# A routed expert layer in which the expert that ranks last by load has no slots of its own

## The chip, the cores and the metric

The kernel runs on one core of one Trainium2 chip. The metric is device microseconds (us) for one execution of the whole program. All times below come from three timed runs of the kernel before and from one profiled execution of it.

## The reference, cut to what matters

The program computes two transformer-like blocks on 256 tokens of width 1024. The change concerns the end of the first block, a layer of 32 experts of which each token uses four:

```python
N_EXPERTS, TOP_K, D_EXPERT = 32, 4, 1024
logits = xt @ w_router + b_router              # 256 tokens x 32 experts
top_logits, top_idx = lax.top_k(logits, TOP_K)
top_w = softmax(top_logits)
# for every expert e, on the tokens that chose it:
gate, up = split(xb @ w_gu[e] + b_gu[e], 2)    # 1024 x 2048 weights, 8 MB
act = (min(gate, 7) * sigmoid(1.702 * gate)) * (clip(up, -7, 7) + 1)
y_e = act @ w_dn[e] + b_dn[e]                  # 1024 x 1024 weights, 4 MB
# y[token] = sum over its four experts of top_w * y_e
```

How many of the 1024 (token, expert) pairs fall to an expert is known only when the router has run. The inputs are drawn from a fixed seed. After the experts come a layer norm and the second block (a pooling layer, a gated delta-rule layer, two wide multilayer perceptrons).

## The kernel before, in words

The program is a long straight line of instructions with one small loop in it. Its stages are: the token mixer of the first block, the router, the experts, and the second block.

**Ranks.** `route` (L680) counts the tokens of each expert and ranks the experts by that count (`rank`, L715). Expert 0 is always given rank 0, so that its weights can be loaded before the router has run. The row `eid` (L721) holds the expert of each rank; the load queue on SP reads one entry of it for each expert (L1080) and fetches that expert's weights by that number. So the order of the work is fixed when the program is built, in terms of ranks, and only the addresses are found at run time.

**Slots.** Each rank has a fixed number of token slots, `cap` (L966): 64 for rank 0, 128 for rank 1, 96 for ranks 2 to 4, 64 for ranks 5 to 14 and 32 for ranks 15 to 31. The text calls an expert by its rank and its slots. An expert with more tokens than slots leaves the rest to a general loop (`For_i`, L1122), which does one pass of 128 slots for each leftover piece, one piece after the other. How many passes there are (`n_over`, L768) and for which experts is found by `leftovers` (L747): `tier` compares the rank with each bound, `base` is the number of slots of the rank, and `f` says whether the count is above it.

**Order.** `_phase_b` (L955) spreads the four kinds of rank evenly over the sequence (`want`, L968) and packs neighbours into units of at most 128 slots (L972). A unit's tokens are gathered together: 32 matmuls with one-hot matrices (L800, L801) make the columns of all its experts. In the sequence below a bar ends a unit:

```
0 | 15 5 16 | 17 6 18 | 1 | 7 19 20 | 8 21 | 2 22 | 9 23 | 10 24 25 | 3 | 11 26 27 | 12 28 | 13 29 | 4 30 | 14 31
```

**One step of the sequence** (loop at L1070) puts on TensorE: the gate and up projection of this expert (`ex_gu`, L844, eight loads of 1 MB each), between its loads the scatter of the expert two steps back (L945) and the activation of the last one (transposes, L864 and L868); then the down projection of the last expert (`ex_down`, L920, four loads of 1 MB), and, when this expert is the first of its unit, the gather for the next unit between these loads.

**Matmul shapes.** An expert with 32 slots uses 32 of the array's 128 columns, so four matmuls run side by side; with 64 slots two run side by side. A 96-slot expert does its gate and up projection as three 32-slot pieces and its down projection one matmul at a time. A 128-slot expert does everything one matmul at a time.

**Loads.** All expert weights go through the one queue on SP into a ring of seven 1 MB buffers (`wpools`, L960). A load is issued when the matmuls of the load seven places earlier are done. Every expert has twelve loads, whatever its slots.

After the last step come the rest of its work, the general loop, and the second block.

Of the kernel before, what the change touches and what calls it, by code (L numbers as in the profile page):

```python
# [9 lines left out]
F32 = mybir.dt.float32  # L10
# [4 lines left out]
OP = mybir.AluOpType  # L15
AX = mybir.AxisListType
# [5 lines left out]
TT = 2  # L22
OFF = -1500
N_TOP, N_BIG = 2, 5
NL = 8
FB = 1
FE = 18
# [8 lines left out]
NO = 3  # L36
N_MID = 10
# [16 lines left out]
class K:  # L54
# [625 lines left out]
    def route(self, pb, p1, first):  # L680

        nc, sm = self.nc, self.sm
        E = N = 32
        wr, br, iota1, pcol = self.rt
        lg, W, M = self.lg, self.W, self.M
        iotaE = self.iotaE
        self.show("lg", lg)
        self.show("Wt", W)

        for tt in range(TT):  # L690
            pp = self.bank([128, N])
            if tt:
                nc.tensor.matmul(pp, self.ones, M[:, 0], start=True, stop=False)
            nc.tensor.matmul(pp, self.upper, M[:, tt], start=tt == 0, stop=True)
            nc.vector.scalar_tensor_tensor(p1[:, tt], pp, 1.0, M[:, tt], op0=OP.add, op1=OP.mult)

        pc = self.bank([N, E + 32])
        for tt in range(TT):
            nc.tensor.matmul(pc[:, :E], self.ones[:, :N], M[:, tt, :E], start=tt == 0, stop=tt == 1)
        for tt in range(TT):  # L700
            nc.tensor.matmul(pc[:, E:], M[:, tt], self.ones[:, :32], start=tt == 0, stop=tt == 1)
        next(first)
        key = self.t(pb, [N, E], F32, "key")
        nc.vector.scalar_tensor_tensor(key, pc[:, :E], 32.0, iotaE[:N, :E], op0=OP.mult, op1=OP.subtract)

        nc.vector.memset(key[:, 0:1], 1e6)
        cc = self.t(pb, [N, 1], F32, "cc")
        nc.vector.tensor_copy(cc, pc[:, E:E + 1])
        kc = self.t(pb, [N, 1], F32, "kc")
        nc.vector.scalar_tensor_tensor(kc, cc, 32.0, pcol, op0=OP.mult, op1=OP.subtract)  # L710
        nc.vector.memset(kc[0:1], 1e6)
        gt = self.t(pb, [N, E], F32, "gt")
        rank = self.t(pb, [N, 1], F32, "rank")
        nc.vector.tensor_scalar(gt, key, kc, None, op0=OP.is_gt)
        nc.vector.tensor_reduce(rank, gt, axis=AX.X, op=OP.add)  # L715
        PP = self.t(pb, [N, 2, E], F32, "PP")
        nc.vector.tensor_scalar(PP[:, 0], iotaE[:N, :E], rank, None, op0=OP.is_equal)
        pe = self.bank([1, E])
        nc.tensor.matmul(pe, pcol, PP[:, 0], start=True, stop=True)
        eid = self.t(pb, [1, 2, E], I32, "eid")  # L720
        nc.vector.tensor_copy(eid[:, 0], pe)  # L721
        fin(first)
        pT = self.t(pb, [N, 2, T], F32, "pTr")
        tab = self.t(pb, [128, 4, TT, E], F32, "tab")

        def permute(z, pos, less=None):

            pr = self.bank([128, 2, TT, E])
            for tt in range(TT):
                for q in range(2):  # L730
                    x = pT[:, 1] if q else pos
                    nc.tensor.matmul(pr[:, q, tt], x[:, tt * 128:tt * 128 + 128], PP[:, z], start=True,
                                     stop=q > 0 or less is None)
                    if q == 0 and less is not None:
                        nc.tensor.matmul(pr[:, q, tt], less[0], less[1], start=False, stop=True)
            nc.vector.tensor_copy(tab[:, 2 * z:2 * z + 2], pr)

        def by_rank():

            ptp = self.bank([N, 2, T])  # L740
            for tt in range(TT):
                nc.tensor.transpose(ptp[:, 0, tt * 128:tt * 128 + 128], p1[:, tt], self.ident)
                nc.tensor.transpose(ptp[:, 1, tt * 128:tt * 128 + 128], W[:, tt], self.ident)
            nc.vector.tensor_copy(pT, ptp)
            permute(0, pT[:, 0])

        def leftovers():  # L747

            tier = self.t(pb, [N, 4], F32, "tier")
            for q, n in enumerate((N_TOP, N_BIG, N_BIG + N_MID, 1)):  # L750
                nc.vector.tensor_scalar(tier[:, q:q + 1], rank, float(n), None, op0=OP.is_lt)
            base = self.t(pb, [N, 1], F32, "base")
            nc.vector.tensor_reduce(base, tier[:, 0:3], axis=AX.X, op=OP.add)
            nc.vector.scalar_tensor_tensor(base, tier[:, 3:4], -2.0, base, op0=OP.mult, op1=OP.add)
            nc.vector.tensor_scalar(base, base, 32.0, 32.0, op0=OP.mult, op1=OP.add)
            f = self.t(pb, [N, 2], F32, "f2")
            nc.vector.tensor_tensor(f[:, 0:1], cc, base, op=OP.is_gt)
            nc.vector.scalar_tensor_tensor(f[:, 1:2], cc, -128.0, base, op0=OP.add, op1=OP.is_gt)
            yield
            pn = self.bank([N, 4])  # L760
            nc.tensor.matmul(pn[:, 0:2], self.upper[:N, :N], f, start=True, stop=True)
            nc.tensor.matmul(pn[:, 2:4], self.ones[:N, :N], f, start=True, stop=True)

            b = self.t(pb, [N, 4], F32, "ib")
            nc.vector.tensor_copy(b, pn)
            nc.vector.tensor_tensor(b[:, 1:2], b[:, 1:2], b[:, 2:3], op=OP.add)
            self.n_over = self.t(pb, [1, 1], I32, "nover")
            nc.vector.tensor_tensor(self.n_over, b[0:1, 2:3], b[0:1, 3:4], op=OP.add)  # L768
            nc.vector.scalar_tensor_tensor(b[:, 0:2], b[:, 0:2], 1.0, f, op0=OP.add, op1=OP.mult)
            P2 = self.t(pb, [N, E], F32, "P2")  # L770
            nc.vector.tensor_scalar(P2, iota1[:N, :E], b[:, 1:2], None, op0=OP.is_equal)
            nc.vector.scalar_tensor_tensor(PP[:, 1], iota1[:N, :E], b[:, 0:1], P2, op0=OP.is_equal, op1=OP.add)
            pos = self.s4([N, T])
            nc.vector.tensor_scalar(pos, pT[:, 0], base, None, op0=OP.subtract)
            less = self.s4([N, 128])
            nc.vector.memset(less, -128.0)
            yield
            pe = self.bank([1, E])
            nc.tensor.matmul(pe, pcol, PP[:, 1], start=True, stop=True)
            nc.vector.tensor_copy(eid[:, 1], pe)  # L780
            permute(1, pos, (less, P2))
            yield
        return pT, PP, eid, tab, by_rank, leftovers
# [171 lines left out]
    def _phase_b(self, st, keep):  # L955
        nc, tc, i = self.nc, self.tc, self.i
        E = 32
        pb = self.pb = st.enter_context(tc.tile_pool(name="pb", bufs=1))
# [5 lines left out]

        order = []
        size = lambda r: 64 if r == 0 else 128 if r < N_TOP else 96 if r < N_BIG else 64 if r < N_BIG + N_MID else 32  # L966
        tiers = [range(0, 1), range(1, N_BIG), range(N_BIG, N_BIG + N_MID), range(N_BIG + N_MID, E)]
        want = [(WA + WB * (j + 0.5) / len(rs)) if n == 1 else (j + 0.5) / len(rs) for n, rs in enumerate(tiers)  # L968
                for j in range(len(rs))]
        flat = [(r, size(r)) for rs in tiers for r in rs]  # L970
        order = [flat[j] for j in sorted(range(E), key=lambda j: (flat[j][0] > 0, want[j]))]
        units, cur = [order[:1]], []  # L972
        for r, cap in order[1:]:
            if sum(c for _, c in cur) + cap > XC:
# [77 lines left out]
        def start():  # L1052

            for tt in range(TT):
                for h in range(2):
                    po = self.bank([128, 512])
                    nc.tensor.matmul(po, pT[:E, 1, tt * 128:tt * 128 + 128], bdn[:, h * 512:h * 512 + 512],
                                     start=True, stop=True)
                    s5 = slice(h * 512, h * 512 + 512)
                    nc.vector.tensor_tensor(po, po, self.g2[:, s5], op=OP.mult)  # L1060
                    nc.vector.scalar_tensor_tensor(ytok[:, tt, s5], ytok[:, tt, s5], ALPHA1, po, op0=OP.mult, op1=OP.add)
                yield

        def others():
            yield from leftovers()
            self.gdn_consts()
            yield
        pend, prev, old, left, pre = [start()] + [iter(())] * NO + [others()], None, None, E, self.pre_c(keep)
        late = []
        for u in range(len(units)):  # L1070
            items = nxt
            for n, (r, cap, xe, off, ow) in enumerate(items):
# [4 lines left out]
                if r:  # L1077

                    with tc.issue_after(self.mid):
                        e = nc.sync.value_load(eid[0:1, 0, r:r + 1], min_val=0, max_val=E - 1)  # L1080
                x = {"n": E - 1 - left}
                fills = []
                if prev:
                    fills = [self.ex_act(prev[0], prev[2], prev[4])]
# [25 lines left out]
                old, prev = prev, (x, e, cap, ow, bcol[:, :, r])  # L1110
        if old:
            fin(self.ex_scatter(old[0], old[2], old[3]))
        x, e, cap, ow, bg = prev
# [788 lines left out]
```

## Time and profile before

| what | value |
|---|---|
| three timed runs, median (lowest to highest) | 2034.7 us (2030.83 to 2046.16) |
| the profiled execution, its own time | 2035.08 us |
| its span from first to last instruction | 2032.3 us |
| busy share of the span: TensorE, VectorE, ScalarE, GpSimd | 91%, 48%, 32%, 1% |
| bytes read from HBM | 575.53 MB |
| mean granted TensorE clock | 0.945 |

The profiled execution lies 2.8 us above its span and 0.4 us above the median. Times inside the program are given from the start of the span. A matmul in float32 shows as two records in the trace, so 8 records of L844 are the four matmuls of one 1 MB load of a 32-, 64- or 128-slot expert, and 24 those of a 96-slot expert. [...]

### The profile page before, as it was taken

The numbers are of one execution on the slowest core, as the hardware profiler recorded it, in microseconds if no ns is written. First come the engines' busy times: TensorE is split into PE (matmuls) and PEld (weight loads), VectorE is DVE, ScalarE is ACT, GpSimd is POOL, SyncE is SP. The second block draws the span as 40 slices with busy tenths as digits, with TensorE's granted clock in tenths as the row PEclk, the third lists the DMA queues.
The fourth block names the chain that finished last, engine by engine and source line by source line (L and its number), as shares of the span: only waits on it lengthen the run. The fifth ranks groups of instructions, "written<-read, shape, count | busy, mean of one in ns | idle before, by whom it ended". The sixth has DMA issues, their size and how long they took to land. (4 is left out here: it accounts for less than half of the span.)

```text
span 2032.3 us, 28434 instructions
## 1 busy us (share of the span) xinstructions
PE 1841.4 (91%) x10991; PEld 1149.6 (57%) x10991; DVE 976.5 (48%) x2179; ACT 647.3 (32%) x1188; POOL 25.0 (1%) x53
## 2 busy tenths in 40 slices
PE   5999989988997899869988898799998899999998
PEld 3988965322431233213322232388997788878997
DVE  4999873313132222212212242556556677766555
ACT  3564541110110111101110210244455466555443
POOL 1000000000000000000000000000000000000000
PEclk9999988978998899989978899999999899999999
DMA  9759577999999999999999999845654222245551
GB/s 340 237 165 355 187 266 294 351 417 398 406 378 417 418 416 417 418 416 395 402 416 417 417 396 418 310 161 192 190 165 134 84 84 68 94 134 192 192 189 42
DMA packets 188057, 578.45 MB, mean 285 GB/s; under 512 B 9736, under 2 KB 89008, under 8 KB 155376
## 3 DMA queue, kind: packets, MB, share of 16 engines
q1 hardware_dynamic: 184960, 568.63, 74.4%
q0 software_dynamic: 2768, 7.92, 1.2%
q8 instruction: 87, 1.43, 0.3%
q14 instruction: 50, 0.41, 0.1%
q10 hardware_dynamic: 192, 0.07, 0.0%
HBM read 575.53 MB, written 1.05 MB: 284 GB/s over the span
## 5 line engine op out<-in xcount | busy, mean ns | idle before, releaser
L844 PE MATMUL pgu<-w,xe 128*32 128x512 f32 (+2 forms) x2416 | 433.7, 653 | 59.5 <-DMA w<-in_w_gu_dram 59.1
L164 DVE TENSOR_TENSOR wsl<-w,wsh 128x1024 fp32r<-128x1024 f32 x256 | 312.3, 1223 | 197.5 <-ACT wsh L160 196.5
L160 ACT CAST wsh<-w 128x1024 fp32r<-128x1024 f32 x256 | 267.8, 1049 | 336.2 <-PE pd L186 197.1
L185 PE MATMUL pd<-a,wsh 128*128 128x256 f32 x1200 | 348.5, 291 | 6.3 <-DVE g_y L1582 3.8
L186 PE MATMUL pd<-a,wsh 128*128 128x256 f32 x1200 | 342.8, 286 | 1.1 <-DVE a L366 1.1
L187 PE MATMUL pd<-a,wsl 128*128 128x256 f32 x1200 | 341.4, 285 | 1.2 <-DVE wsl L164 1.2
L844 PEld LDWEIGHTS pgu<-w,xe 128*32 128x32 f32 (+2 forms) x2416 | 106.3, 124 | 316.0 <-issue 177.5
L920 PE MATMUL pb<-w,a 128*32 128x512 f32 (+3 forms) x992 | 221.6, 657 | 36.1 <-DMA w<-in_w_dn_dram 32.6
L185 PEld LDWEIGHTS pd<-a,wsh 128*128 128x128 f32 x1200 | 232.0, 194 | 16.3 <-issue 5.2
L186 PEld LDWEIGHTS pd<-a,wsh 128*128 128x128 f32 x1200 | 231.8, 193 | 5.3 <-issue 2.1
L187 PEld LDWEIGHTS pd<-a,wsl 128*128 128x128 f32 x1200 | 231.3, 193 | 1.5 <-DVE wsl L164 1.5
L889 ACT ACTIVATE esg<-eg 128x256 f32<-128x256 f32 x52 | 21.7, 417 | 401.7 <-DVE eg L888 401.7
L920 PEld LDWEIGHTS pb<-w,a 128*32 128x32 f32 (+3 forms) x992 | 56.4, 131 | 155.4 <-issue 113.1
L947 DVE TENSOR_TENSOR a<-pb,a 128x512 f32<-128x512 f32 x128 | 83.6, 687 | 120.1 <-PE pb L945 120.1
L931 DVE TENSOR_TENSOR a<-pb,g2p 128x512 f32<-128x512 f32 x28 | 19.4, 691 | 250.1 <-PE pb L920 250.0
L207 PE MATMUL pb<-wsh,a 128*128 128x512 f32 x320 | 125.5, 392 | 0.0
L208 PE MATMUL pb<-wsh,a 128*128 128x512 f32 x320 | 125.5, 392 | 0.0
L209 PE MATMUL pb<-wsl,a 128*128 128x512 f32 x320 | 124.9, 390 | 0.0
L945 PE MATMUL pb<-a,S 64*128 64x512 f32 (+2 forms) x256 | 94.6, 661 | 20.4 <-DVE a L931 17.2
L852 ACT COPY a<-pgu 128x512 f32<-128x512 f32 x52 | 29.4, 587 | 242.3 <-PE pgu L844 242.3
L386 DVE SCALAR_TENSOR_TENSOR a<-yp,V,a 128x228 f32<-128x228 f32 (+26 forms) x240 | 97.9, 461 | 0.4
L790 DVE TENSOR_SCALAR ow<-iota,tab 128x128 f32<-128x128 f32 x62 | 18.8, 344 | 157.4 <-PE pb L934 157.4
(501 smaller groups left out, 2150.6 us busy)
## 6 DMA issues: line engine op xcount, KB each, us to landing
w<-in_w_gu_dram SPq DMA_DIRECT2D x254, 1024.0 KB, 13.6
w<-in_w_dn_dram SPq DMA_DIRECT2D x124, 1024.0 KB, 12.2
w<-in_mlp_w_dram SPq DMA_DIRECT2D x64, 1024.0 KB, 5.3
w<-in_w_mod_dram SPq DMA_DIRECT2D x24, 1024.0 KB, 7.0
w<-in_w_in_dram SPq DMA_DIRECT2D x24, 1024.0 KB, 9.5
w<-in_gdn_w_in_dram SPq DMA_DIRECT2D x16, 1024.0 KB, 5.6
w<-in_ple_gate_w_dram SPq DMA_DIRECT2D x8, 1024.0 KB, 5.0
w<-in_w_b_dram SPq DMA_DIRECT2D x4, 1024.0 KB, 11.6
```

The lines of the kernel that those rows point to most:

```text
L160: nc.scalar.copy(h, src)
L164: nc.vector.tensor_tensor(l, src, h.bitcast(F32), op=OP.subtract)
L185: nc.tensor.matmul(ps, wh[:, k], xh[:, k], start=k == 0, stop=False)
L186: nc.tensor.matmul(ps, wh[:, k], xl[:, k], start=False, stop=False)
L187: nc.tensor.matmul(ps, wl[:, k], xh[:, k], start=False, stop=k == KT - 1)
L207: nc.tensor.matmul(acc, xh[:, k, sl], wh[:, a, s5], start=first and a == 0, stop=False)
L208: nc.tensor.matmul(acc, xl[:, k, sl], wh[:, a, s5], start=False, stop=False)
L209: self.last_mm = nc.tensor.matmul(acc, xh[:, k, sl], wl[:, a, s5], start=False, stop=last and a == na - 1).ins
L386: nc.vector.scalar_tensor_tensor(cv[:, c, s:], yp[:, c, :T - s], cw(k, c), cv[:, c, s:], op0=OP.mult, op1=OP.add)
L844: nc.tensor.matmul(o, xe[:, k, sl], w[c], start=k == 0, stop=k == KT - 1, skip_group_check=True)
L920: nc.tensor.matmul(o, act[:, k], w[a][:, h * 512:h * 512 + 512], start=first, stop=last, skip_group_check=True)
L945: nc.tensor.matmul(po, S[p, tt * 128:tt * 128 + 128], y[p, c0:c0 + 512], start=True, stop=True)
```

## The change

The number of ranks with slots becomes 31 (`N_ALL`). Rank 31 is left out of the sequence, so its twelve loads, its gather columns, its projections, activation and scatter are no longer in the straight part of the program. In `leftovers` one more bound is compared, and the slots of rank 31 are zero, so a token of that rank would make the general loop run. The sequence of the remaining ranks is spread and packed anew. The bias `b_dn` of all experts is added elsewhere and stays.

```diff
+N_ALL = 31
...
-            tier = self.t(pb, [N, 4], F32, "tier")
-            for q, n in enumerate((N_TOP, N_BIG, N_BIG + N_MID, 1)):
+            tier = self.t(pb, [N, 5], F32, "tier")
+            for q, n in enumerate((N_TOP, N_BIG, N_BIG + N_MID, N_ALL, 1)):
                 nc.vector.tensor_scalar(tier[:, q:q + 1], rank, float(n), None, op0=OP.is_lt)
             base = self.t(pb, [N, 1], F32, "base")
-            nc.vector.tensor_reduce(base, tier[:, 0:3], axis=AX.X, op=OP.add)
-            nc.vector.scalar_tensor_tensor(base, tier[:, 3:4], -2.0, base, op0=OP.mult, op1=OP.add)
-            nc.vector.tensor_scalar(base, base, 32.0, 32.0, op0=OP.mult, op1=OP.add)
+            nc.vector.tensor_reduce(base, tier[:, 0:4], axis=AX.X, op=OP.add)
+            nc.vector.scalar_tensor_tensor(base, tier[:, 4:5], -2.0, base, op0=OP.mult, op1=OP.add)
+            nc.vector.tensor_scalar(base, base, 32.0, None, op0=OP.mult)
...
-        tiers = [range(0, 1), range(1, N_BIG), range(N_BIG, N_BIG + N_MID), range(N_BIG + N_MID, E)]
+        tiers = [range(0, 1), range(1, N_BIG), range(N_BIG, N_BIG + N_MID), range(N_BIG + N_MID, N_ALL)]
...
-        order = [flat[j] for j in sorted(range(E), key=lambda j: (flat[j][0] > 0, want[j]))]
+        order = [flat[j] for j in sorted(range(N_ALL), key=lambda j: (flat[j][0] > 0, want[j]))]
...
-        pend, prev, old, left, pre = [start()] + [iter(())] * NO + [others()], None, None, E, self.pre_c(keep)
+        pend, prev, old, left, pre = [start()] + [iter(())] * NO + [others()], None, None, N_ALL, self.pre_c(keep)
...
-                x = {"n": E - 1 - left}
+                x = {"n": N_ALL - 1 - left}
```

The sequence of the changed kernel, again with a bar at the end of a unit, has 15 units as before:

```
0 | 15 5 16 | 6 17 | 1 | 18 7 19 | 20 8 21 | 2 | 9 22 23 | 10 24 | 3 | 11 25 26 | 12 27 28 | 13 | 4 29 | 14 30
```

The lines of the changed kernel are numbered two higher. At the end of the sequence the load queue on SP, before, reads the last entry of `eid` and then issues eight loads from `w_gu` and two times four from `w_dn`; here are its first rows:

```order
L896 DMA w_8561<-in_w_dn_dram 128x2x1024
L1080 TENSOR_LOAD eid_3312
L1080 ISA x2
L825 ISA
L825 DMA w_8577<-in_w_gu_dram 128x2048
L825 ISA
```

In the changed kernel, at the same place, the queue goes straight to the four last loads from `w_dn`, and then to the weights of the second block:

```order
L898 DMA w_8572<-in_w_dn_dram 128x2x1024
L898 ISA
L898 DMA w_8614<-in_w_dn_dram 128x2x1024
L898 ISA
L898 DMA w_8620<-in_w_dn_dram 128x2x1024
L898 ISA
L898 DMA w_8626<-in_w_dn_dram 128x2x1024
L898 ISA
L898 DMA w_8632<-in_w_dn_dram 128x2x1024
L1241 DMA plew_8678<-in_ple_proj_dram 128x1024
```

Eight loads of `w_gu` and four of `w_dn` are gone, with the read of `eid` ahead of them, and nothing else on this queue.

The second place is on TensorE, where the down projection of rank 1 (128 slots, `pb` with 512 columns) begins. Before, the last gate and up projection ahead of it is that of rank 7 with 64 slots (`pgu`, 64x512), and the gather behind it (`oh`) has 96 columns:

```order
L844 MATMUL pgu_4674<-w_4798,xe_4472 64x512
L844 MATMUL pgu_4675<-w_4798,xe_4472 64x512
L844 MATMUL pgu_4674<-w_4798,xe_4472 64x512
L844 MATMUL pgu_4675<-w_4798,xe_4472 64x512
L920 MATMUL pb_4807<-w_4809,a_4719 128x512
L920 MATMUL pb_4808<-w_4809,a_4719 128x512
L920 MATMUL pb_4807<-w_4809,a_4719 128x512
L920 MATMUL pb_4808<-w_4809,a_4719 128x512
L800 MATMUL pb_4815<-oh_4662,a_3025 128x96
```

In the changed kernel the expert between is rank 18 with 32 slots, and the gather has 128 columns:

```order
L846 MATMUL pgu_4555<-w_4615,xe_4348 32x512 x4
L846 MATMUL pgu_4555<-w_4636,xe_4348 32x512 x4
L846 MATMUL pgu_4555<-w_4657,xe_4348 32x512 x4
L846 MATMUL pgu_4555<-w_4678,xe_4348 32x512 x4
L922 MATMUL pb_4686<-w_4688,a_4599 128x512
L922 MATMUL pb_4687<-w_4688,a_4599 128x512
L922 MATMUL pb_4686<-w_4688,a_4599 128x512
L922 MATMUL pb_4687<-w_4688,a_4599 128x512
L802 MATMUL pb_4694<-oh_4538,a_3025 128x128
```

So a 32-slot expert has taken the place of a 64-slot one between the two halves of rank 1.

## Rows read from the trace of the kernel before

**Rows 1.** The page: busy time by engine, and DMA share and rate in 40 slices.

```profile
PE 1841.4 (91%) x10991; PEld 1149.6 (57%) x10991; DVE 976.5 (48%) x2179; ACT 647.3 (32%) x1188; POOL 25.0 (1%) x53
...
DMA  9759577999999999999999999845654222245551
GB/s 340 237 165 355 187 266 294 351 417 398 406 378 417 418 416 417 418 416 395 402 416 417 417 396 418 310 161 192 190 165 134 84 84 68 94 134 192 192 189 42
```

**Rows 2.** DMA issues by source: count, KB each, median us from issue to landing.

```profile
w<-in_w_gu_dram SPq DMA_DIRECT2D x254, 1024.0 KB, 13.6
w<-in_w_dn_dram SPq DMA_DIRECT2D x124, 1024.0 KB, 12.2
...
a<-in_w_dn_dram SPq DMA_DIRECT2D x3, 1024.0 KB, 6.3
a<-in_w_gu_dram SPq DMA_DIRECT2D x3, 512.0 KB, 9.4
...
a<-in_w_dn_dram SPq DMA_DIRECT2D x2, 512.0 KB
...
lg<-in_w_gu_dram SPq DMA_DIRECT2D x1, 512.0 KB
```

**Rows 3.** What TensorE waited for from 400 to 1300 us: total, times, longest.

```profile
PE pgu L844 <- DMA w<-in_w_gu_dram: 59.1, 61, 1.5
PE pb L920 <- DMA w<-in_w_dn_dram: 32.6, 40, 1.7
```

**Rows 4.** Busy time by engine in stretches of the expert stage; last: clock, DMA, GB/s.

```profile
460.00:480.00 20.00, 19.10 (x104) 7.26 (x104) 7.41 (x33) 1.86 (x4) 0.47 (x2) 0.98 0.98 368
540.00:550.00 10.00, 10.00 (x64) 4.57 (x62) 0.69 (x1) 4.44 (x9) 0.00 (x0) 1.00 0.94 359
580.00:600.00 20.00, 20.00 (x112) 8.77 (x114) 8.38 (x22) 3.38 (x8) 0.00 (x0) 1.00 0.85 320
600.00:700.00 100.00, 78.19 (x416) 21.76 (x406) 21.94 (x55) 9.91 (x22) 0.00 (x0) 0.90 1.02 417
700.00:800.00 100.00, 94.49 (x570) 34.55 (x574) 26.84 (x68) 13.48 (x30) 0.00 (x0) 0.98 1.02 417
800.00:920.00 120.00, 91.93 (x474) 24.65 (x470) 26.59 (x67) 10.17 (x23) 0.00 (x0) 0.88 1.02 417
920.00:1000.00 80.00, 79.43 (x488) 30.66 (x478) 22.21 (x60) 13.63 (x30) 0.00 (x0) 0.99 0.99 392
1160.00:1200.00 40.00, 39.54 (x290) 13.82 (x289) 12.44 (x52) 9.45 (x20) 0.00 (x0) 0.96 0.99 393
1200.00:1280.00 80.00, 70.92 (x330) 22.01 (x330) 21.83 (x53) 5.87 (x13) 0.00 (x0) 0.94 1.02 416
```

**Rows 5.** TensorE in order of time around rank 1: start, us, line, tiles, records.

```profile
513.46 10.57 PE L844 MATMUL pgu<-w,xe 128*128 128x512 f32 x24
...
528.99 13.90 PE L844 MATMUL pgu<-w,xe 128*128 128x512 f32 x32
...
568.90 1.94 PE L844 MATMUL pgu<-w,xe 128*64 128x512 f32 x8
570.78 3.70 PE L920 MATMUL pb<-w,a 128*128 128x512 f32 x8
...
588.22 1.06 PE L844 MATMUL pgu<-w,xe 128*32 128x512 f32 x8
...
590.58 1.98 PE L945 MATMUL pb<-a,S 128*128 128x512 f32 x4
```

**Rows 6.** TensorE in order of time on a 32-slot expert: in brackets the wait before.

```profile
426.74 1.06 PE L844 MATMUL pgu<-w,xe 128*32 128x512 f32 x8 [1.36 <-DMA w<-in_w_gu_dram]
...
436.70 1.94 PE L844 MATMUL pgu<-w,xe 128*32 128x512 f32 x8 [0.57 <-DMA w<-in_w_gu_dram]
```

**Rows 7.** VectorE in order of time where the ranks are made.

```profile
310.65 0.31 DVE L751 TENSOR_SCALAR tier<-rank 32x1 f32<-32x1 f32 x4
...
313.39 0.18 DVE L721 CAST eid<-pb 1x32 int32<-1x32 f32 x1 [2.31 <-PE pb L719]
```

**Rows 8.** TensorE in 10 us stretches, granted clock and rate of the loads.

```profile
440.00:450.00 10.00, 10.00 (x46) 5.23 (x39) 0.00 (x0) 2.29 (x5) 0.00 (x0) 0.50 1.03 418
```

## The prediction

> **What bounds the kernel now.** I read the page first. Its busy line puts TensorE at 91% and the other engines at half or less, which looks like a TensorE kernel. Its slices say something else for one long stretch: from the ninth slice (some 406 us) to the 25th (1270 us) the DMA share stands at 9 tenths or more and the rate near 417 GB/s, while before and after the rate changes from slice to slice [rows 1]. That stretch is the expert stage. So I went to the views that show what waits for what in it.
>
> The table of stretches shows the rate at 416 or 417 GB/s over whole stretches in which TensorE is busy for 78, 94, 92 and 71 of 100, 100, 120 and 80 us, thus whether TensorE has much work or little [rows 4]. The view of waits shows the same from TensorE's side: from 400 to 1300 us it waited 59.1 us for gate and up weights and 32.6 us for down weights, in 101 short pieces [rows 3]. On a 32-slot expert the picture is plain: four matmuls of 1.06 us in all, then 1.36 us of waiting for the next megabyte [rows 6]. In most of the stage the time is the bytes of the weights over 417 GB/s. The exceptions are five stretches below 400 GB/s, where TensorE is busy for all or nearly all of the time [rows 4]. There the ring of seven buffers is full of loads that TensorE has not used, so the queue stands. I put the lost time of each as its length times (1 - rate / 417): 460 to 480 us, 2.4 us; 540 to 550, 1.4; 580 to 600, 4.7; 920 to 1000, 4.8; 1160 to 1200, 2.3 us. The sum is 15.6 us.
>
> **First part: what is removed.** The issues count 254 and 124 loads of 1 MB; with the early loads of the first expert and half-size ones (four halves make two, three and two halves make four) that is 256 from `w_gu` and 128 from `w_dn`, exactly 32 times eight and 32 times four [rows 2]. Rank 31 therefore costs 12 x 1024 KB = 12.58 MB, and the general loop loaded nothing. The loads of the other ranks move up in the same queue. At 417 GB/s the removal is 12.58 MB / 417 = **30.2 us**, as long as the queue stays as full as before. The bounds from the nearest rows are 12.58 / 418 = 30.1 us and, at the rate of the worst stretch, 12.58 / 320 = 39.3 us; I take 417, the rate of the long stretches. The TensorE work of rank 31 goes too: 12 groups of 1.06 us and a scatter. It lies between waits for loads, so it is not counted a second time. The last four experts of the sequence keep their shapes (96, 32, 64, 32), so the end of the stage and the preparation of the second block in it should look as before: 0.
>
> **Second part: what is moved.** The new packing decides how far TensorE falls behind at the big experts. I go through those whose neighbours change.
>
> (a) Rank 2 (96 slots). The down projection of an expert stands behind the gate and up projection of the next one, and the gather beside it is as wide as the unit to come. Before, rank 22 with 32 slots stood between the two halves of rank 2; now it is rank 9 with 64 slots, and the unit to come behind rank 2's first half has 128 columns instead of 96. That is just what rank 3 has before: alone in its unit, followed by 11 (64 slots) and two small ones. Before, rank 2's stretch, 700 to 800 us, lost nothing at 417 GB/s, and rank 3's, 920 to 1000 us, lost 4.8 us [rows 4]. So I charge rank 2 **+4.8 us**, between 0 and 4.8.
>
> (b) Rank 1 (128 slots) kept TensorE from 513.46 to 542.89 us with its first half (the last row starts at 528.99 and lasts 13.90), and from 570.78 to 588.22 us with its second half and a gather; between them stood rank 7 with 1.94 us for each load [rows 5]. Now rank 18 with 1.06 us stands there, 8 x (1.94 - 1.06) = 7.0 us less at the worst point. The two losses here are 1.4 and 4.7 us. The first precedes the changed place and stays; of the second I take most as gone: **-4.0 us**, between 0 and -4.7. The gather grows from 96 to 128 columns, the shape of the gather at 540 us, and I count that inside this range.
>
> (c) Rank 4 is now preceded by 13 (64 slots) instead of 29 (32), so a 64-slot down projection follows its first half, 4 x 0.88 = 3.5 us more at the point where 1160 to 1200 us lost 2.3 us. I charge **+2.0 us**, between 0 and 3.5.
>
> (d) Rank 3 keeps its neighbours in kind; the first units lose one 32-slot column set. 0, between -2.4 (the loss at 460 us gone) and +2.4 (doubled).
>
> **Third part: the ranks.** One comparison more on a 32x1 column. Four of them took 0.31 us together, and behind them VectorE waits 2.31 us for TensorE before it can write `eid` [rows 7]. The added 0.1 us lies in that wait: 0. Without that cover it would be 0.1 us. The added slots of `tier` feed only the count of leftovers, and the loop is passed by as before as long as that count is zero.
>
> **Sum.** -30.2 + 4.8 - 4.0 + 2.0 = -27.4 us. The profiled execution took 2035.08 us, so the forecast is 2007.7 us. The median of the timed runs is 0.4 us below the profiled one, which I leave out.
>
> **The rivals.**
>
> *The new neighbours eat the gain (B).* For it: TensorE is busy for 95 to 100% of each stretch below 400 GB/s [rows 4], and its clock is not always full. [...] In the stretch of rank 3 the mean clock was 0.99, so the 4.8 us there are at full clock. [...] Price: (a) and (c) at their upper ends, (b) at nothing, (d) at +2.4, thus +4.8 + 3.5 + 2.4 = 10.7, and 3 us more for slow-clock work, four loads at 0.88 us: 30.2 - 14 = 16 us of gain, 2019 us. Against it: 417 GB/s over rank 2 with TensorE at 94 of 100 us shows that such a place can be passed without loss.
>
> *TensorE is the bound after all (C).* Then removing rank 31 is worth its TensorE time: 12 x 1.06 plus four scatter matmuls at about half of 1.98 for two, 2.0, thus some 15 us, and the time is 2020 us. For it: 91% busy. Against it: 91.7 us of waiting for weights in the stage, none of which a TensorE bound would have.
>
> *The general loop runs (D).* If rank 31 has a single token, one pass of 128 slots is done behind everything else: 29.4 us for the first half, 17.4 us for gather and second half, 4.0 us for the scatter [rows 5], and about 9 us for the first loads and the activation that nothing covers (my choice, between the 6.3 us of a lone load and the 13.6 us of a queued one [rows 2]), together 60 us. The time is 2007.7 + 60 = 2068 us, slower. It decides from one token on. Against it: routing the reference's inputs of its default seed gives the counts 99, 90, 89, 78, 64 for ranks 1 to 5 and 1 and 0 for ranks 30 and 31; expert 15 is chosen by no token, and its logit lies at least 0.377 below the fourth best of every token. The trace agrees as far as it can: the counts fit all slots, and the loop loaded nothing. For it: the trace doesn't show a count, and other inputs have a token there.
>
> *The losses go away (E).* A shorter sequence could leave less lag everywhere: (a) 0, (b) -4.7, (d) -2.4, thus 37 us of gain and 1998 us.
>
> **How the numbers follow.** The forecast, with its own range of 2000 to 2014 us, has 0.73; B 0.11; C 0.05; D 0.06; E 0.05. About 1%, 20 us, is what a measurement of this kernel can tell from no change. Faster by over 1% means below 2014.3 us: the forecast and E, 0.78. Within 1%: B and C, 0.16. Slower: D, 0.06. The range leaves out D and half of E's far side: 1998 to 2020 us.
>
> **What would show it.** The changed profile should show 12.58 MB less from HBM, 246 and 120 loads of 1 MB in place of 254 and 124, and the last loads of the stage some 27 us earlier, with the second block unchanged in length. Step (a) is right if the rate drops below 400 GB/s after rank 2's first half; (b) if the drop after rank 1's second half is below 2 us; (c) if the drop at rank 4 grows. The prediction is wrong in kind if L844 of the general loop has records, if the rate falls below 400 GB/s in stretches with small experts alone, or if the second block takes back what the stage gave.

## The result and the profile after

The changed kernel took 2005.07 us in the median of four runs (2002.63 to 2011.09), the kernel before 2033.01 us in the median of four. The ratio is 0.9844, with a 95% interval of 0.9819 to 0.9869, so it is faster by 1.3 to 1.8%. The forecast was 2007.7 us with a range of 1998 to 2020 us. Two later comparisons of the same two kernels gave 0.9845 and 0.9840.

The total is close to the forecast, but its parts are not. One term was too small by 8 us, and others made up for it. The profiled execution shows it; it took 2011.09 us, the slowest of the four, 24.0 us below the profiled execution of before.

The page of the changed kernel, lines as in [rows 1] and [rows 2]:

```profile
PE 1826.2 (91%) x10881; PEld 1149.3 (57%) x10881; DVE 971.1 (48%) x2165; ACT 645.2 (32%) x1185; POOL 24.9 (1%) x53
...
GB/s 341 226 162 354 188 260 299 343 417 417 398 408 401 410 416 411 416 416 418 416 417 418 336 393 415 259 154 188 189 166 124 84 85 70 94 147 189 189 189 43
...
HBM read 562.95 MB, written 1.05 MB: 281 GB/s over the span
...
w<-in_w_gu_dram SPq DMA_DIRECT2D x246, 1024.0 KB, 14.1
w<-in_w_dn_dram SPq DMA_DIRECT2D x120, 1024.0 KB, 11.9
```

The twelve loads are gone: 246 and 120 in place of 254 and 124, and 562.95 MB in place of 575.53, which is 12.58 MB. TensorE is at 91% as before. The new thing is one slice of the rate, the 23rd, at 336 GB/s. Before, no slice between the ninth and the 25th was below 378 [rows 1].

The first load behind the expert weights (`plew`) is issued 25.2 us earlier, where the prediction said some 27; before, then changed:

```profile
1275.57 0.46 SPq L1239 DMA_DIRECT2D plew<-in_ple_proj_dram  x1
...
1250.37 1.61 SPq L1241 DMA_DIRECT2D plew<-in_ple_proj_dram  x1
```

From the first matmul on it (1300.59 and 1279.09 us) to the end of the span are 731.7 and 730.2 us, so the second block has kept its length.

The stretches of the changed kernel that answer to [rows 4] (columns as there: start and end, length, busy time and count by engine, then TensorE's granted clock as a share of its full speed, DMA share and GB/s):

```profile
480.00:540.00 60.00, 57.68 (x254) 24.77 (x251) 17.38 (x48) 9.34 (x20) 0.00 (x0) 1.00 1.00 400
560.00:600.00 40.00, 33.41 (x179) 9.72 (x179) 11.61 (x29) 3.65 (x8) 0.00 (x0) 0.91 1.01 404
640.00:660.00 20.00, 19.09 (x68) 6.51 (x66) 5.37 (x11) 0.42 (x1) 0.00 (x0) 0.77 0.93 357
720.00:800.00 80.00, 76.44 (x426) 29.58 (x418) 25.12 (x64) 13.99 (x31) 0.00 (x0) 1.00 1.01 412
800.00:1100.00 300.00, 249.29 (x1344) 76.34 (x1346) 69.08 (x172) 31.66 (x71) 1.94 (x4) 0.90 1.02 417
1100.00:1160.00 60.00, 60.00 (x330) 21.26 (x330) 16.83 (x54) 10.99 (x22) 1.12 (x3) 0.86 0.89 342
1160.00:1180.00 20.00, 20.00 (x134) 7.86 (x122) 5.17 (x22) 5.58 (x12) 0.00 (x0) 1.00 0.99 385
```

By the measure of the prediction (length times 1 - rate / 417) the losses are 2.4 and 1.2 us at rank 1, 2.9 us at rank 8, 1.0 us at rank 2, and 10.8 + 1.5 = 12.3 us at rank 4. Rank 3 lies in the 300 us at 417 GB/s and loses nothing. These are single profiles, and not all of the losses come again, as the part on the prediction shows. The queue was still full almost everywhere, and TensorE waited for it as in [rows 3]:

```profile
PE pgu L846 <- DMA w<-in_w_gu_dram: 47.9, 51, 1.5
PE pb L922 <- DMA w<-in_w_dn_dram: 31.4, 37, 2.5
```

What happened at rank 4 is in the order of time on TensorE (start, us, line, tiles, shape, records):

```profile
1105.89 10.57 PE L846 MATMUL pgu<-w,xe 128*64 128x512 f32 x48
1116.39 1.06 PE L922 MATMUL pb<-w,a 128*32 128x512 f32 x8
...
1123.17 1.07 PE L922 MATMUL pb<-w,a 128*32 128x512 f32 x8
...
1124.53 11.73 PE L1316 MATMUL pb<-a,ident 4*128 4x512 f32 x16
1136.19 4.92 PE L846 MATMUL pgu<-w,xe 128*32 128x512 f32 x24
...
1163.41 1.94 PE L922 MATMUL pb<-w,a 128*64 128x512 f32 x8
```

Line 1316 belongs to the first step of `pre_c`, the preparation of the second block. It spreads four rows of parameters over 128 partitions with eight matmuls that have only four rows (`4*128`), 16 records. It needs no weights, so while it runs no buffer of the ring comes free; the rate was 272 GB/s from 1130 to 1140 us and 222 in the 10 us behind. In the changed kernel it stands directly behind the gather for the unit 4 29 and directly ahead of the three-piece gate and up projection of rank 4. From 1116 to 1136 us TensorE used only four of the loads in the ring, and then it took up rank 4 with 4.92 us for the first load and 2.78 us for the next ones, where a load needs 2.5 us to arrive (1 MB at the 417 GB/s of [rows 4]). The down projection of rank 13 begins at 1163 us, behind most of the loss. Before, the same step came one small expert after the gather: four of its records between the down projections of rank 13 (1.12 us for each two), and twelve behind them:

```profile
1158.39 5.41 PE L1314 MATMUL pb<-a,ident 4*128 4x512 f32 x12
1163.74 4.48 PE L844 MATMUL pgu<-w,xe 128*32 128x512 f32 x24
```

Its 16 records took 7.65 us there, in place of 11.73.

### The profile page after: what moved, and what is told of

It reads as the page before. It is cut to its first block, busy times and chain, and to the rows that moved or that the text cites. A ratio compares the mean times of both kernels' runs of the same rounds, so it can differ in the third digit from the quotient of the medians.

```text
span 2009.3 us, 28145 instructions
## 1 busy us (share of the span) xinstructions
PE 1826.2 (91%) x10881; PEld 1149.3 (57%) x10881; DVE 971.1 (48%) x2165; ACT 645.2 (32%) x1185; POOL 24.9 (1%) x53
## 3 DMA queue, kind: packets, MB, share of 16 engines
HBM read 562.95 MB, written 1.05 MB: 281 GB/s over the span
## 5 line engine op out<-in xcount | busy, mean ns | idle before, releaser
L846 PE MATMUL pgu<-w,xe 128*32 128x512 f32 (+2 forms) x2352 | 420.1, 647 | 47.9 <-DMA w<-in_w_gu_dram 47.9
L922 PE MATMUL pb<-w,a 128*32 128x512 f32 (+3 forms) x960 | 217.4, 663 | 37.4 <-DMA w<-in_w_dn_dram 31.4
```

Of the source, the lines that this page charges most:

```text
L846: nc.tensor.matmul(o, xe[:, k, sl], w[c], start=k == 0, stop=k == KT - 1, skip_group_check=True)
L922: nc.tensor.matmul(o, act[:, k], w[a][:, h * 512:h * 512 + 512], start=first, stop=last, skip_group_check=True)
```

## The experiments

Each is compared with the kernel before on the same chip. The median of before was 2038.8 us beside the first four kernels, 2038.9 beside the next three and 2039.2 beside the last three.

**The changed kernel again.** No edit.

> The changed kernel once more, for a second profile. Theory P (the preparation of the second block, sixteen records of L1316, 11.7 us of TensorE, stands straight behind the gather 4 29 and ahead of rank 4): the rate of the loads falls below 300 GB/s around rank 4's first half again, and some 7 to 11 us of the queue's time are lost there. Rival C4 (only the slow clock of that one execution made the loss): with TensorE at full clock there, the loss is at most 5 us. Both: 2002 to 2011 us.

Measured: 2007.38 us (2000.78 to 2012.08), ratio 0.9845, interval 0.9809 to 0.9882. Its stretch at rank 4, in the table of stretches:

```profile
1100.00:1160.00 60.00, 59.77 (x356) 21.07 (x356) 19.40 (x69) 12.33 (x25) 1.12 (x3) 0.91 0.93 364
1130.00:1140.00 10.00, 10.00 (x53) 2.19 (x51) 0.60 (x2) 1.55 (x3) 0.00 (x0) 0.64 0.77 301
1140.00:1150.00 10.00, 10.00 (x84) 2.92 (x80) 3.89 (x9) 0.30 (x1) 0.00 (x0) 1.00 0.80 283
```

The loss is there again, 60 x (1 - 364 / 417) = 7.6 us in place of 10.8, with a higher clock; L1316 took 9.60 us. A third profile of this kernel, from the last comparison below, has 60 x (1 - 337 / 417) = 11.5 us, with 13.37 us for L1316:

```profile
1100.00:1160.00 60.00, 59.09 (x327) 21.17 (x330) 17.15 (x55) 11.00 (x22) 1.12 (x3) 0.86 0.86 337
```

So the loss comes in every profile of this order, and it is smaller where L1316 is shorter. Rival C4 isn't settled by this: no profile of this order has the full clock there. If L1316 took its 7.65 us of before, some 2 us of the 7.6 would go as well, an estimate.

**The old sequence without rank 31.**

```diff
-        tiers = [..., range(N_BIG + N_MID, N_ALL)]
+        tiers = [..., range(N_BIG + N_MID, E)]
-        order = [flat[j] for j in sorted(range(N_ALL), ...)]
+        order = [flat[j] for j in sorted(range(E), ...) if flat[j][0] < N_ALL]
```

> Rank 31 is taken out of the sequence of before, and nothing else moves; the last unit is rank 14 alone. Theory L (the twelve loads alone are worth 30.2 us, the rest of the difference is packing): 2033 - 30 = 2003 us, within 3 us, and rank 4's stretch loses some 2 us as before. Rival N (the new packing is the better one, and the loads are worth less than 30 us): 2008 us or more.

Measured: 2008.7 us (2005.8 to 2009.73), ratio 0.9851 (0.9823 to 0.9879), thus 0.0149 x 2038.8 = 30.4 us less than before, with an interval of 25 to 36 us. The loads are worth what theory L says. The time itself lies where rival N put it, at 2008 us or more, but only because the kernel before took 2038.8 us here and not 2033. The new packing as a whole is worth nothing that can be measured, 0.9851 against 0.9845. Leaving out one expert also moves the countdown that places L1316, so here it meets a gather too, but a small expert follows it; the rows are in order of time on TensorE, then from the table of stretches:

```profile
1127.30 1.06 PE L922 MATMUL pb<-w,a 128*32 128x512 f32 x8 [0.82 <-DMA w<-in_w_dn_dram]
...
1128.66 12.88 PE L1316 MATMUL pb<-a,ident 4*128 4x512 f32 x16
1141.47 1.94 PE L846 MATMUL pgu<-w,xe 128*32 128x512 f32 x8
```
```profile
1130.00:1160.00 30.00, 30.00 (x118) 9.10 (x118) 11.82 (x48) 6.67 (x13) 0.64 (x2) 0.72 0.94 367
...
900.00:1000.00 100.00, 93.38 (x552) 33.53 (x554) 25.47 (x66) 14.02 (x32) 0.00 (x0) 0.94 1.00 403
```

The step takes even longer, 12.88 us, but 1.94 us for a load is less than the 2.5 us of a load, and the loss is 30 x (1 - 367 / 417) = 3.6 us instead of 12.3. My figure of some 2 us for this place was too low.

**The preparation two experts earlier.**

```diff
-                if 2 < left <= NPRE:
+                if left in (3, 6):
```

> The changed kernel with the first step of the preparation of the second block (L1316) two experts earlier, ahead of rank 28 among small experts. Theory P: the loss at rank 4 goes from 10.6 us to 2 to 4 us, nothing above 3 us appears at rank 28, and the time is 5 to 9 us below the changed kernel's, 1997 to 2000 us. Rival G (the 64-slot down projection of rank 13 and the gathers are what stops the loads at rank 4): the loss stays at 7 us or more and the time within 2 us of the changed kernel's.

Measured: 1996.42 us (1993.79 to 1997.57), ratio 0.9791 (0.9763 to 0.9819). Beside the changed kernel's 2007.38 us in the same comparison that is 11 us less, more than the 5 to 9 I expected. The same stretch of time, and the new place of the step ahead of rank 28, in the table of stretches:

```profile
1060.00:1100.00 40.00, 36.86 (x166) 9.97 (x167) 9.75 (x20) 6.44 (x12) 0.00 (x0) 0.87 1.00 407
1100.00:1160.00 60.00, 56.57 (x385) 20.93 (x383) 16.37 (x66) 10.55 (x23) 0.64 (x2) 1.00 1.02 416
```

The stretch with rank 13's down projection and rank 4 runs at 416 GB/s, at full clock, though the packing is that of the changed kernel to the last column. So the 64-slot down projection, to which the prediction gave this loss, is not its cause (rival G). At the new place 40 x (1 - 407 / 417) = 1.0 us is lost.

**Loads without work.** The methods of an expert return early or skip their matmuls when `bare` is set.

```diff
-                x = {"n": E - 1 - left}
+                x = {"n": E - 1 - left, "bare": r == 24}
```

> The kernel before, in which rank 24 (32 slots, in the middle of the sequence) keeps its twelve loads but none of its projections, activation and scatter; its tokens get nothing from it. Theory L (the loads set the pace of the stage): no gain, between -3 and +2 us against the kernel before. Rival T (TensorE sets the pace): some 15 us less, 2018 us.

Measured: 2034.97 us, ratio 0.9982 (0.9964 to 1.0000), thus 0 to 7 us less than before. In the table of stretches:

```profile
800.00:900.00 100.00, 68.58 (x345) 21.56 (x344) 22.53 (x59) 8.20 (x19) 0.00 (x0) 0.84 1.02 417
```

With rank 24's work gone TensorE is busy for 69 of 100 us and the rate stays at 417. By the ratio it is some 4 us faster, just past the 3 us that I gave theory L, and well short of the 15 of rival T.

**Work without loads.** Rank 24 multiplies by the resident tile `g2` in place of weights.

```diff
+            elif x.get("own"):
+                w = [self.g2[:, c % 2 * 512:c % 2 * 512 + 512] for c in range(4)]
...
+            w = [self.g2, self.g2] if x.get("own") else ...
```

> The kernel before, in which rank 24 keeps all its matmuls and evictions but loads no weights: it multiplies by a resident tile instead, so its tokens get something else. Theory L (the loads set the pace): the whole of the twelve loads is gained less what TensorE then falls behind, 24 to 31 us below the kernel before. Rival T (TensorE sets the pace): no gain beyond 5 us.

Measured: 2014.12 us (2008.16 to 2014.84), ratio 0.9870 (0.9843 to 0.9897), thus 26.5 us less than before (21 to 32). The work takes some time in which the queue stands with a full ring; in the table of stretches one place near rank 24 is new:

```profile
860.00:870.00 10.00, 7.06 (x36) 2.76 (x36) 5.67 (x16) 1.31 (x3) 0.00 (x0) 1.00 0.65 267
```

It loses 10 x (1 - 267 / 417) = 3.6 us, about what lies between 26.5 and 30.2; TensorE waited 2.94 us there for an activation on VectorE (L894), while the queue waited up to 8.5 us for a buffer. The two kernels together say where an expert's time is: its loads without its work cost all of it within 7 us, its work without its loads some 4 us.

**The preparation moved in the kernel before.** The edit of pre_moved, with 32 experts.

> The kernel before, with all 32 ranks, and the first step of the preparation of the second block (L1314) moved as in pre_moved; it then stands ahead of rank 13. Theory P (that step costs only where it meets the gather for rank 4's unit with no small expert between): rank 4's loss of 2.3 us goes and a small one may appear at 13; -3 to +2 us against the kernel before. Rival M (the step is better placed there in any kernel): 5 us or more faster than before.

Measured: 2036.8 us, ratio 0.9992 (0.9978 to 1.0007): no difference. The loss changes its place, in the table of stretches:

```profile
1100.00:1120.00 20.00, 20.00 (x64) 6.16 (x64) 5.19 (x12) 2.73 (x6) 0.00 (x0) 0.75 0.93 345
1160.00:1200.00 40.00, 39.09 (x306) 14.13 (x302) 15.73 (x59) 6.29 (x14) 0.00 (x0) 1.00 1.02 417
```

Rank 4's 2.3 us are gone, and 20 x (1 - 345 / 417) = 3.5 us appear at rank 13, a 64-slot expert that now follows the step directly, at a mean clock of 0.75. So there is nothing to gain from that edit in the old sequence. What it repairs is the meeting of the step with the gather and rank 4, which only the new sequence has.

**One pass of the general loop.**

```diff
-N_ALL = 31
+N_ALL = 30
```

> The changed kernel with one rank fewer still: rank 30, which has one token, has no slots, so the general loop makes one pass. The prediction's rival D priced a pass at 60 us and an expert's loads at 30: 2007 - 30 + 60 = 2037 us, the same as the kernel before within 10 us. If the pass hides behind other work it is 2010 us or less; if more of it is bare than I counted, 2050 us or more.

Measured: 2043.11 us (2032.49 to 2048.56), ratio 1.0013 (0.9988 to 1.0037), the same as before. The pass, in order of time on TensorE, from its first transpose to the first matmul of the second block:

```profile
1242.93 0.20 PE L1129 MATMUL pb<-ident,a 16*128 16x16 f32 x1 [1.13 <-DVE a L1353]
...
1253.42 29.67 PE L846 MATMUL pgu<-w,xe 128*128 128x512 f32 x64
1282.92 1.91 PE L866 MATMUL pb<-ident,a 128*128 128x128 f32 x16
1286.15 13.97 PE L922 MATMUL pb<-w,a 128*128 128x512 f32 x32 [1.32 <-issue]
1299.96 0.38 PE L936 MATMUL pb<-ident,ow 128*128 128x128 f32 x2
1300.81 3.70 PE L947 MATMUL pb<-a,S 128*128 128x512 f32 x8 [0.46 <-ACT S L938]
1305.69 3.70 PE L1234 MATMUL pd<-plew,pT 128*128 128x512 f32 x8 [1.19 <-issue]
```

It takes 1305.7 - 1242.9 = 62.8 us for one token, of which the gate and up projection alone is 29.67 and the loads hide nothing of it, since TensorE sets the pace here: from 1260 to 1280 us it was busy for 20.00 of 20 us, with the loads at 263 GB/s. The rival's 60 us was a fair price.

**A narrower interval, and the step earlier still.** The changed kernel, pre_moved, and a third place for the step (`left in (3, 7)`, ahead of rank 27, behind the gather of unit 13).

> The changed kernel beside the next two, for a narrower interval: 0.984 to 0.986 of the kernel before.

> The same edit as pre_moved, for a narrower interval. Theory P: 0.978 to 0.981 of the kernel before, its interval clear of the changed kernel's. Rival: the first gain was scatter between runs, and the two intervals lie on each other.

> The step one expert earlier still, ahead of rank 27 (32 slots), right after rank 12's first half and the gather of unit 13. Theory P (any place among small experts does, one behind a gather less so): as pre_moved, or up to 3 us slower.

Measured: 2006.99 us (2000.09 to 2007.87, ratio 0.9840, 0.9812 to 0.9867), 1998.42 us (1996.37 to 1999.11, ratio 0.9804, 0.9779 to 0.9828) and 1996.86 us (1992.91 to 2003.45, ratio 0.9811, 0.9784 to 0.9838). The intervals of the first two overlap by 0.0016, where theory P wanted them apart; both carry the spread of the kernel before. But all five runs of pre_moved lie below all five of the changed kernel, and so did all four in the first comparison (1997.57 at most against 2000.78 at least). Moving the step is worth 8.6 us by these medians and 11 us by the first ones. Its two early places can't be told apart by time; in the profile the place behind a gather loses more, 100 x (1 - 404 / 417) = 3.1 us against 1.0, as theory P said:

```profile
1000.00:1100.00 100.00, 89.36 (x394) 27.84 (x396) 24.34 (x54) 12.94 (x27) 1.87 (x4) 0.79 1.00 404
```

The version with the step moved is faster than both kernels of this case.

## Why the prediction was right, and where it was not

**What bounds the stage: right.** The reading of [rows 3] and [rows 4] against the 91% of [rows 1] is confirmed from both sides, by loads_alone and work_alone. Rival C, 15 us for the TensorE work, falls with them.

**First part, 30.2 us: right.** keep_order, which does this and moves nothing else but the countdown of the preparation, gives 30.4 us with an interval of 25 to 36.

**First part, "the preparation of the second block in it should look as before: 0": wrong, and with it the size of (c).** I counted the shapes of the last four experts and left out the preparation that is woven between them by a countdown of experts. It keeps its place ahead of rank 4, but its neighbour changed: in the old sequence the gather for rank 4's unit and the step were one 32-slot expert apart, in the new one they touch. (c) stood at +2.0 us with 3.5 as its upper bound; the profile shows 12.3 - 2.3 = +10.0 us. The cause that (c) named, the 64-slot down projection, costs next to nothing once the step is elsewhere.

Not all of the 10.0 us is the order. The old sequence can lose more at rank 4 too: in loads_alone, whose edit lies some 300 us earlier, the slices with rank 4 (the 23rd and 24th) stand at 406 and 369 GB/s, 50.8 x (2 - 775 / 417) = 7.2 us, where the kernel before has 417 and 396 [rows 1], 2.6 us. The 16 records took 9.57 us there, in place of 7.65:

```profile
GB/s 343 227 163 356 193 260 295 352 417 395 407 375 417 417 416 417 418 416 417 418 416 416 406 369 418 312 163 186 187 167 143 84 84 68 94 133 191 191 189 42
```

So the term is not the same in every execution. That moving the step takes the whole loss away is shown by pre_moved; how the loss divides between the new neighbours and the slow clock (0.50 from 1130 to 1140 us in the changed kernel) was not tried.

**(a), +4.8 us: too much, and its source misread.** Rank 2 lost 1.0 us, and rank 3, for which (d) said 0, lost nothing either, a change of -4.8 us. The 4.8 us that (a) took over from rank 3 are no fixed cost of its neighbours. In before_moved, with the same sequence up to there, the two slices with rank 3 (the 19th and 20th) stand at 417 and 416 GB/s in place of 395 and 402 [rows 1], 0.1 us lost in place of 4.5:

```profile
GB/s 341 230 162 343 192 259 306 354 417 399 398 384 417 417 416 418 418 416 417 416 416 392 414 415 418 314 154 189 187 168 141 84 84 68 94 137 192 190 188 42
```

The two executions differ in how rank 3 begins. In the kernel before the clock was 0.50 from 910 to 920 us, and the first three loads of rank 3 took 10.42 us; in before_moved they took 7.93, as 72 such records of the changed kernel did from 1155.55 us on at a clock of 1.00:

```profile
910.00:920.00 10.00, 9.10 (x34) 2.25 (x37) 2.67 (x4) 0.00 (x0) 0.00 (x0) 0.50 1.01 422
916.38 10.42 PE L844 MATMUL pgu<-w,xe 128*32 128x512 f32 x72
...
915.23 7.93 PE L844 MATMUL pgu<-w,xe 128*32 128x512 f32 x72
```

With the scatter just ahead (3.75 against 1.95 us) that is 4.3 us, about the difference of the two losses. So "the 4.8 us there are at full clock" was wrong: the stretch from 920 us on has a mean of 0.99, but the delay was made just ahead of it. keep_order loses 3.4 us from 900 to 1000 us, at a mean clock of 0.94.

**(b), -4.0 us: right in kind.** Rank 1 lost 2.4 + 1.2 = 3.6 in place of 6.1 us, -2.5.

**(d), 0 within 2.4: too narrow.** The loss at 460 us is gone, -2.4 us, and rank 3's with it, -4.8. But 2.9 us appeared at rank 8, at a mean clock of 0.77, where I expected nothing, and the later profiles of this kernel have it too (341 and 354 GB/s). Only small experts stand there, which the prediction named as a sign of being wrong in kind. The four matmuls of a down load of a 32-slot expert took 1.94 us there instead of 1.06, at a clock of 0.50 from 630 to 640 us and with a gather between them. At 440 us the same clock went with 418 GB/s [rows 8]; here 357 followed, in a stretch without any big expert.

The terms as measured are -30.2 + 10.0 + 1.0 - 2.5 - 4.8 - 2.4 + 2.9 = -26.0 us in the profile; the sum of the prediction was -27.4. The queue agrees: from the first matmul of the experts (315.98 and 316.95 us) to the issue of `plew` are 959.6 and 933.4 us, 26.2 us less. The profiled executions differ by 24.0 and the medians by 27.9 us. The error of +8.0 us at (c) stood against -6.6 us from all the others. That they cancelled was luck, the more so as the losses at ranks 3 and 4 differ between executions of the old sequence (4.5 and 0.1 us, 2.6 and 7.2); the 30.2 us for the loads carried the forecast.

**Third part, the ranks: not visible**, as forecast. **Rival B** came true in mechanism at rank 4 (the work around a big expert grew, with the clock at 0.50 from 1130 to 1140 us), but not in its price, since other places gained. Its 0.88 us for a load at the slow clock is 1.94 - 1.06 [rows 6]; that there would be four of them was an estimate that no run shows, and in their place the records of the step took 11.73 - 7.65 = 4.1 us more. **Rival D** stayed away because rank 31 has no token in these inputs; one_pass shows what a single token there costs, 62.8 us, so that the kernel would be some 35 us slower than before instead of 28 us faster, an estimate from 62.8 - 27.9.

## What to carry to other kernels

In a stage that the load queue paces, price a removed load at its bytes over the stage's rate, and then look for the places where TensorE has work that needs no load. A gather and the preparation step side by side, ahead of a big expert, lost 8 to 12 us here; with one small expert between, or elsewhere, 1 to 4, and once 7, where the records of the step took 9.57 us. When an item is taken out of a sequence, list everything that is placed by counting items, also what belongs to the next stage, and see what it now stands next to. A total that comes out right is worth a check term by term: here 9 to 11 us were still to be had by one line. A loss read from one profile can belong to that execution alone (rank 3's was 4.5 us with the clock at 0.50 as it began, and 0.1 us in before_moved): read it in a second one before charging it to the order of the work.

## What the runs showed of the hardware that was not expected

TensorE was busy for the whole of a stretch and yet at a granted clock of 0.50. In the changed kernel's table of stretches:

```profile
1110.00:1120.00 10.00, 10.00 (x60) 4.22 (x56) 0.52 (x1) 1.98 (x4) 0.00 (x0) 1.00 1.03 413
1120.00:1130.00 10.00, 10.00 (x46) 4.89 (x46) 1.31 (x5) 5.00 (x10) 0.64 (x2) 0.84 1.01 419
1130.00:1140.00 10.00, 10.00 (x28) 2.98 (x30) 0.00 (x0) 2.39 (x5) 0.00 (x0) 0.50 0.65 272
```

The clock fell at some 1127 us, while it ran the 16 records of L1316 (from 1124.53 us), of four rows each, and it had waited for nothing from 1100 us on. They took 11.73 us here, 9.60 and 13.37 us in the other profiles of the same kernel, 12.88 us in keep_order, and 7.65 us in the kernel before, where the clock was 1.00 up to 1162 us and 0.50 from 1164 to 1166, behind the last of them. The stretches that hold their end, or begin behind it, are below full clock in other profiles too: 0.64 from 1130 to 1140 us in again, 0.72 from 1130 to 1160 in keep_order, 0.75 from 1100 to 1120 in before_moved. The 0.50 of [rows 8] came behind 10 us in which TensorE was busy for 6.00; here it came after 27 us without a wait. So neither waiting ahead of it nor the busy column alone tells the clock. What made it fall was not tried.
